# A decoder layer on one core: reordering the seven-product units of the second feed-forward product, and moving the input squares

## The chip, the cores and the metric

The kernel runs on one core of one Trainium2 chip. Its time is device microseconds of an execution, the median of several runs. Before the change three runs gave 1564.54 us in the median (1560.53 to 1565.82).

## What is computed

One layer of a decoder, for 256 tokens of width 2048, in float32. The reference, cut to what matters:

```
u = rms_norm(x, pre_mix_gain)
z = u @ w_in                       # 2048 -> q, k, v, conv value and gate, two mixer gates (7 x 2048)
o = rms_norm(diff_attention(rope(q), rope(k), v, lam)) * (1 - 0.2)   # 8 heads, causal
c = c_val * sigmoid(c_gate)        # then a causal depthwise filter of 31 taps
c = silu(layer_norm(conv31(c))) @ w_conv_out + b
m = sigmoid(ga) * o + sigmoid(gc) * c
h = x + rms_norm(m @ w_out)
u = rms_norm(h, pre_ff_gain)
f = square(relu(u @ w_ff1)) @ w_ff2      # 2048 -> 8192 -> 2048
out = h + rms_norm(f)
```

## The kernel before, in words

**Products.** Each float32 operand is split into a high part of the type fp32r and a low part, the rest; a product is made of three matmuls (high x high, low x high, high x low). A weight comes from memory in chunks of 128 x 2048 numbers (1 MB). A chunk goes through four steps: a DMA on SP's queue into one of three buffers `raw` (L137); a cast on ScalarE into one of three buffers `wh` (L143); a subtraction on VectorE into one of three buffers `wl` (L149), below called the lo-split; and the matmuls. `fill()` (L195) traces the next chunks until three are alive, `done()` (L214) gives one back and calls `fill()`. A raw buffer can be loaded again when its cast and its lo-split have read it. `ws_pair` (L266) takes two chunks, 2 x 32 matmuls, for two column blocks of an output; `as_block` and `as_part` (L281) take four chunks for 512 columns of both token tiles.

**Order.** All is traced in program order, and the library's planner then sets each engine's order by priority (program order, shifted by `high_priority(offset)`) and by its own estimate of when operands are ready. On the chip each engine works off its order. `pin` (`keep_in_program_order`) ties an instruction behind the one that was traced just before it on the same engine.

**Lead-in.** The first two chunks and the input are loaded in pieces and multiplied at once (L395 to L410). Then `done()`, the load of `vec`, `done()`, which trace the third, fourth and fifth chunk; then the squares of the input (L425), their sums `xss` (L427 to L429), a matmul with `ones` (L431), two small ones (L434) and the reciprocal roots `rb` and `rt` (L435). A loop over 16 column pairs follows (L478 to L487): `ws_pair`, the copy-out `z` (`ws_sum`, L278 and L279, two buffers), a multiplication by `rb` (L482), a sigmoid (L483), and a filter of 31 taps on VectorE with low priority (L471).

**Second feed-forward product.** It is done in four stages q. In each, eight `ws_pair` make the squared activations `g` of 2048 hidden columns, in `sc` (L844); then two blocks m of 1024 output columns are made with `fast_pair` (L770; in the last stage the second block is made with `as_block`). A `fast_pair` goes over four groups of 512 hidden rows in the order 0, 2, 1, 3. Groups 2 and 3 are plain: two chunks each of 24 matmuls (L815 to L817). Groups 0 and 1 are units of seven products A1 to A7 in place of eight, after Strassen and Winograd: the two raw chunks of a unit are w11, w21 (first) and w12, w22 (second), four sums are made of them on VectorE, and of the activations too (`put_fast`, L760). Seven halves of a weight buffer are cast (L159) and lo-split (L160), in four parts that each take one `wh` and `wl` buffer (`fast_part`, L168):

| part | first half | second half | also made |
|---|---|---|---|
| 0 | w11 for A1 | t1 = w11 + w12 for A5 | w12 += w22 |
| 1 | w12 for A7 | t2 = w12 + w11 for A6 | |
| 2 | w21 for A2 | t4 = t2 + w21 for A4 | |
| 3 | w22 for A3 | | both raw buffers given back |

Each product is 6 matmuls of 512 columns (L793 to L795). A1, A5, A7 and A6 have accumulators of their own (`own`), which ScalarE and VectorE copy out after the second unit (L798 to L803); A2, A4 and A3 add to those of the plain chunks, which are copied out at the end (L819 to L822). All eight banks of PSUM are used by one `fast_pair`, and the next takes the same ones over. From the second stage on, the result is added to `acc` by two DMAs on POOL's queue (L825).

Of the kernel before, what the change touches and what calls it, by code (L numbers as in the profile page):

```python
# [11 lines left out]
F32 = mybir.dt.float32  # L12
# [47 lines left out]
def tile_layer(ctx, tc, x, x_t, pre, vecs, lams, rope_t, subln, b_conv, post_mix, post_ff,  # L60
# [107 lines left out]
    def fast_part(part, i):  # L168
        state["next"] += 1
        state["live"] += 1  # L170
        w11, w21 = quads(raw_tile(i))
        w12, w22 = quads(raw_tile(i + 1))
        wt = (whp.tile([P, CHUNK], F32R, name="wh"), wlp.tile([P, CHUNK], F32R, name="wl"))
        queue.append(wt)

        def new_sum(name, a, b):
            sums[name] = sump.tile([P, 2, 512], F32, name="sum")
            return add(sums[name], a, b)

        if part == 0:  # L180
            split_sum(wt, 0, w11)
            split_sum(wt, 1, new_sum("t1", w11, w12))
            add(w12, w12, w22)
        elif part == 1:
            split_sum(wt, 0, w12)
            split_sum(wt, 1, new_sum("t2", w12, w11))
        elif part == 2:
            split_sum(wt, 0, w21)
            split_sum(wt, 1, new_sum("t4", sums["t2"], w21))
        else:  # L190
            split_sum(wt, 0, w22)
            release_raw(i)
            release_raw(i + 1)

# [71 lines left out]
    def ws_pair(acts):  # L266
        ps = new_ps()
        for j in range(2):
            wh, wl = take()
            for k in range(KT):  # L270
                nc.tensor.matmul(ps[:, j], wh[:, k * P:(k + 1) * P], acts.both(k), start=(k == 0), stop=False)  # L271
            for k in range(KT):
                nc.tensor.matmul(ps[:, j, S:], wl[:, k * P:(k + 1) * P], acts.hi(k), start=False, stop=(k == KT - 1))  # L273
            done()
        return ps
# [136 lines left out]
    done()  # L412
    pin(nc.sync.dma_start(vec, vecs))
    done()

    def vcol(ct, r):
        return vec[:, ct, r:r + 1]
# [4 lines left out]
    with tc.high_priority(offset=CHAIN):  # L422
        for j in range(4):
            sq = xsp.tile([P, 4, S], F32, name="xsq", bufs=2) if j else xss
            pin(nc.scalar.activation(sq, xt[:, 4 * j:4 * j + 4], AF.Square))  # L425
            if j:
                pin(nc.vector.tensor_tensor(xss, xss, sq, op=ALU.add))  # L427
        pin(nc.vector.tensor_tensor(xss[:, 0:2], xss[:, 0:2], xss[:, 2:4], op=ALU.add))
        pin(nc.vector.tensor_tensor(xss[:, 0], xss[:, 0], xss[:, 1], op=ALU.add))  # L429
        pb = aux_ps()[:, 0:S]  # L430
        nc.tensor.matmul(pb, ones, xss[:, 0], start=True, stop=True)  # L431
        pc = aux_ps()[:, 0:NT]
        for t in range(NT):
# [14 lines left out]
    pin(nc.sync.dma_start(rope_sb, rope_t))  # L448
    sub8 = lnp.tile([P, VD], F32, name="sub8")
    pin(nc.sync.dma_start(sub8, subln.partition_broadcast(P)))  # L450
    lam_in = lnp.tile([P, 4, HD], F32, name="lam_in")
    pin(nc.sync.dma_start(lam_in, lams.partition_broadcast(P)))
# [25 lines left out]
    for ct in range(KT):  # L478
        ps = ws_pair(ua) if ct else lead_ps
        z = tmpp.tile([P, 2, S], F32, name="z")  # L480
        ws_sum(z, ps)
        nc.vector.tensor_tensor(z, z, rb2, op=ALU.mult)  # L482
        nc.scalar.activation(z[:, 1], z[:, 1], AF.Sigmoid, bias=vcol(ct, V_GG))  # L483
# [250 lines left out]
    sump = ctx.enter_context(tc.tile_pool(name="sump", bufs=2))  # L734
# [35 lines left out]
    def fast_pair(ga, q, m):  # L770
# [11 lines left out]
        for kc in FF_ORDER:  # L782
            if kc < FAST:
                for pair in ((A1, A5), (A7, A6), (A2, A4), (A3,)):
                    wh, wl = take()
                    for half, a in enumerate(pair):
                        ps = own[a] if a in own else shared[a]
                        for i in range(2):
# [4 lines left out]
                            nc.tensor.matmul(ps, g[:, 0, a], wh[:, sl], start=first, stop=False)  # L793
                            nc.tensor.matmul(ps, g[:, 0, a], wl[:, sl], start=False, stop=False)  # L794
                            nc.tensor.matmul(ps, g[:, 1, a], wh[:, sl], start=False, stop=last)  # L795
# [8 lines left out]
            else:  # L804
                for i in range(2):
                    wh, wl = take()
                    for kk in range(4):
                        k = kc * 4 + kk
                        sl = slice(kk * 512, (kk + 1) * 512)
                        for t in (1, 0):  # L810
# [4 lines left out]
                            nc.tensor.matmul(ps, ga.hi(k, a, b), wh[:, sl], start=first, stop=False)  # L815
                            nc.tensor.matmul(ps, ga.hi(k, a, b), wl[:, sl], start=False, stop=False)  # L816
                            nc.tensor.matmul(ps, ga.lo(k, a, b), wh[:, sl], start=False, stop=last)  # L817
# [19 lines left out]
    for q in range(NQ):  # L837
        ga = Mixed()
        for j in range(KT // 2):
# [4 lines left out]
            sc = fin2.tile([P, 8, P], F32, name="sc")  # L844
# [106 lines left out]
```

## Time and profile before

| | |
|---|---|
| runs, median | 1564.54 us |
| the profiled execution | 1565.17 us, span 1563.4 us |
| TensorE (PE) busy | 1530.4 us |
| its weight loads (PEld) | 1299.7 us |
| VectorE (DVE) busy | 1272.5 us |
| ScalarE (ACT) busy | 769.1 us |
| memory traffic | 306.31 MB, mean 196 GB/s |
| second product, four stages | from 932.85, 1110.06, 1288.48 and 1465.97 us on |

Times in rows are microseconds from the start of the span. A row of the timeline has the start, the length, the engine and the line, and in brackets how long the engine had been idle and what ended it. In the chain of waits a piece counts only until the next piece begins, so a matmul of a back-to-back row stands there with its pitch and not with its modelled length.

### The profile page before, as it was taken

The page shows a single profiled execution, that of the slowest core. Times are in us where ns is not written, and L with a number is a line of the kernel's source. Part 1 is how long each engine was busy: PE and PEld are TensorE (multiplying, and loading weights), DVE is VectorE, ACT ScalarE, POOL GpSimd, SP SyncE. Part 2 cuts the span into 40 slices and gives each one's busy share as a digit, 9 for nine tenths or more (in the row PEclk, how much of TensorE's full clock was granted, in tenths as well). Part 3 has the DMA queues.
Part 4 walks back from the last instruction along what each step waited for, and adds up shares of the span by engine and source line. Part 5 has one row for each costly group of instructions (what it writes and reads, how often), then busy time and mean ns, then how long its engine had stood idle before and what let it go on. Part 6 is the DMA issues. An engine that isn't in the chain of part 4 may idle for free.

```text
span 1563.4 us, 19364 instructions
## 1 busy us (share of the span) xinstructions
PE 1530.4 (98%) x7746; PEld 1299.7 (83%) x7746; DVE 1272.5 (81%) x1609; ACT 769.1 (49%) x812; POOL 17.9 (1%) x44
## 2 busy tenths in 40 slices
PE   9899999999999999999999999999999999899997
PEld 8788888888888888888887887788877888688876
DVE  7899999999999996956547888867887779877775
ACT  7344454646554545734446545544445445544452
POOL 0000000000000000000000000000000000000000
PEclk9999999999999999999999999999999999999999
DMA  8455555544444555575555645555366535575572
GB/s 303 179 192 190 189 188 187 186 166 176 175 167 179 204 200 188 191 269 187 188 191 194 230 148 194 217 211 190 137 220 230 222 136 215 191 267 189 218 253 82
DMA packets 47450, 306.31 MB, mean 196 GB/s; under 512 B 5376, under 2 KB 5504, under 8 KB 12672
## 3 DMA queue, kind: packets, MB, share of 16 engines
q1 hardware_dynamic: 43920, 289.61, 51.0%
q0 software_dynamic: 3008, 14.68, 3.7%
q8 instruction: 60, 0.98, 0.2%
q10 hardware_dynamic: 432, 0.79, 0.2%
q14 instruction: 30, 0.25, 0.0%
HBM read 295.62 MB, written 4.19 MB: 192 GB/s over the span
## 4 chain that ended last, share of the span: by engine, by line
PE 86%; DVE 6%; DMA 5%; ACT 2%; issue 1%; SPq 0%; DVEq 0%; ACTq 0%
PE ps L271 29%; PE ps L273 15%; PE ps L287 10%; PE ps L288 10%; PE ps L289 10%; DMA raw<-in_w_f_dram 4%; PE ps L816 2%; PE ps L817 2%; DVE wl L160 2%; PE ps L815 2%; DVE wl L149 2%; ACT wh L143 1%; DVE sum L165 1%; PE ps L793 1%; PE ps L795 1%; PE ps L794 1%
## 5 line engine op out<-in xcount | busy, mean ns | idle before, releaser
L143 ACT CAST wh<-raw 128x2048 fp32r<-128x2048 f32 (+2 forms) x264 | 467.8, 1780 | 550.2 <-PE ps L271 181.3
L149 DVE TENSOR_TENSOR wl<-raw,wh 128x2048 fp32r<-128x2048 f32 (+2 forms) x264 | 560.6, 2129 | 193.2 <-ACT wh L143 187.8
L271 PE MATMUL ps<-act,wh 128*128 128x512 f32 x1984 | 480.9, 393 | 4.9 <-DVE z L279 4.6
L271 PEld LDWEIGHTS ps<-act,wh 128*128 128x128 f32 x1984 | 365.4, 189 | 76.0 <-issue 4.7
L273 PEld LDWEIGHTS ps<-act,wl 128*128 128x128 f32 x1984 | 256.4, 191 | 9.9
L273 PE MATMUL ps<-act,wl 128*128 128x256 f32 x1984 | 264.0, 284 | 0.0
L289 PE MATMUL ps<-wh,act 128*128 128x512 f32 x624 | 244.0, 391 | 0.0
L287 PE MATMUL ps<-wh,act 128*128 128x512 f32 x624 | 243.7, 391 | 0.0
L288 PE MATMUL ps<-wl,act 128*128 128x512 f32 x624 | 243.3, 390 | 0.0
L471 DVE SCALAR_TENSOR_TENSOR y_all<-c,vec,y_all 128x256 f32<-128x256 f32 x480 | 210.1, 483 | 0.0
L289 PEld LDWEIGHTS ps<-wh,act 128*128 128x128 f32 x624 | 117.1, 188 | 24.3
L287 PEld LDWEIGHTS ps<-wh,act 128*128 128x128 f32 x624 | 117.2, 188 | 24.1
L288 PEld LDWEIGHTS ps<-wl,act 128*128 128x128 f32 x624 | 117.2, 188 | 23.7
L815 PE MATMUL ps<-wh,g 128*128 128x512 f32 x224 | 89.0, 397 | 8.4 <-ACT wh L143 8.4
L816 PE MATMUL ps<-wl,g 128*128 128x512 f32 x224 | 90.2, 403 | 4.4 <-DVE wl L149 4.0
L159 ACT CAST wh<-raw 128x1024 fp32r<-128x1024 f32 x56 | 58.8, 1051 | 66.6 <-PE ps L271 26.7
L817 PE MATMUL ps<-wh,g 128*128 128x512 f32 x224 | 88.4, 395 | 0.0
L160 DVE TENSOR_TENSOR wl<-raw,wh 128x1024 fp32r<-128x1024 f32 x56 | 68.3, 1222 | 11.7 <-PE ps L273 10.8
L794 PE MATMUL ps<-wl,gs 128*128 128x512 f32 x196 | 76.4, 390 | 0.0
L795 PE MATMUL ps<-wh,gs 128*128 128x512 f32 x196 | 76.3, 389 | 0.0
L793 PE MATMUL ps<-wh,gs 128*128 128x512 f32 x196 | 72.9, 391 | 2.0 <-ACT wh L159 2.0
L159 ACT CAST wh<-sum 128x1024 fp32r<-128x1024 f32 x42 | 44.0, 1049 | 47.1 <-DVE sum L165 47.1
(215 smaller groups left out, 1295.5 us busy)
## 6 DMA issues: line engine op xcount, KB each, us to landing
raw<-in_w_f_dram SPq DMA_DIRECT2D x124, 1024.0 KB, 4.9
raw<-in_w_q_dram SPq DMA_DIRECT2D x16, 1024.0 KB, 4.9
raw<-in_w_k_dram SPq DMA_DIRECT2D x16, 1024.0 KB, 4.9
raw<-in_w_v_dram SPq DMA_DIRECT2D x16, 1024.0 KB, 4.9
raw<-in_w_ga_dram SPq DMA_DIRECT2D x16, 1024.0 KB, 4.8
raw<-in_w_gc_dram SPq DMA_DIRECT2D x16, 1024.0 KB, 4.8
raw<-in_w_co_dram SPq DMA_DIRECT2D x16, 1024.0 KB, 4.8
raw<-in_w_o_dram SPq DMA_DIRECT2D x16, 1024.0 KB, 4.8
```

Source lines behind the costliest of these rows:

```text
L143: i = nc.scalar.copy(wh[:, a:b], raw[:, a:b])
L149: i = (eng or nc.vector).tensor_sub(wl[:, a:b], raw[:, a:b], wh[:, a:b].bitcast(F32))
L159: nc.scalar.copy(hi, src)
L271: nc.tensor.matmul(ps[:, j], wh[:, k * P:(k + 1) * P], acts.both(k), start=(k == 0), stop=False)
L273: nc.tensor.matmul(ps[:, j, S:], wl[:, k * P:(k + 1) * P], acts.hi(k), start=False, stop=(k == KT - 1))
L287: nc.tensor.matmul(ps, acts.hi(k, a, b), wh[:, sl], start=(k == 0), stop=False)
L288: nc.tensor.matmul(ps, acts.hi(k, a, b), wl[:, sl], start=False, stop=False)
L289: nc.tensor.matmul(ps, acts.lo(k, a, b), wh[:, sl], start=False, stop=(k == KT - 1))
L471: i = nc.vector.scalar_tensor_tensor(y, c[:, j:j + S], vcol(ct, V_DW + j), y, op0=ALU.mult, op1=ALU.add)
L815: nc.tensor.matmul(ps, ga.hi(k, a, b), wh[:, sl], start=first, stop=False)
L816: nc.tensor.matmul(ps, ga.hi(k, a, b), wl[:, sl], start=False, stop=False)
L817: nc.tensor.matmul(ps, ga.lo(k, a, b), wh[:, sl], start=False, stop=last)
```

## The change

- Parts 0 to 3 of a unit hold A1 and A2, A7 and A3, A5 and A6, and A4. Part 0 reads only the first raw chunk; part 1 makes all four sums and its two halves and gives both raw buffers back; parts 2 and 3 only cast and lo-split sums that are there. The matmuls take the products in that order. `sum` has three buffers instead of two, `sc` one instead of two.
- All matmuls of `fast_pair` are pinned.
- The copy-outs of the first of a block's two column halves (L819, L820) are traced after the first of the last two plain chunks.
- Lead-in: one chunk is traced by `fill()`, then `vec`, then the squares (with a higher priority), then the two `done()`, then the first `ws_pair` of the loop, pinned, and only then the matmuls with `ones`, the first of them pinned. The loads of the rope table, `sub8` and `lam_in` are tied behind the gate of the fifth column pair.

```diff
     def fast_part(part, i):
         state["next"] += 1
         state["live"] += 1
-        w11, w21 = quads(raw_tile(i))
-        w12, w22 = quads(raw_tile(i + 1))
+        if part < 2:
+            w11, w21 = quads(raw_tile(i))
+            w12, w22 = quads(raw_tile(i + 1))
...
         if part == 0:
             split_sum(wt, 0, w11)
-            split_sum(wt, 1, new_sum("t1", w11, w12))
-            add(w12, w12, w22)
+            split_sum(wt, 1, w21)
         elif part == 1:
-            split_sum(wt, 0, w12)
-            split_sum(wt, 1, new_sum("t2", w12, w11))
-        elif part == 2:
-            split_sum(wt, 0, w21)
-            split_sum(wt, 1, new_sum("t4", sums["t2"], w21))
-        else:
-            split_sum(wt, 0, w22)
+            new_sum("t1", w11, w12)
+            split_sum(wt, 0, add(w12, w12, w22))
+            split_sum(wt, 1, w22)
+            new_sum("t2", w12, w11)
+            new_sum("t4", sums["t2"], w21)
             release_raw(i)
             release_raw(i + 1)
+        elif part == 2:
+            split_sum(wt, 0, sums["t1"])
+            split_sum(wt, 1, sums["t2"])
+        else:
+            split_sum(wt, 0, sums["t4"])
...
-    def ws_pair(acts):
+    def ws_pair(acts, pinned=False):
...
     vec = const.tile([P, KT, NV], F32, name="vec")
-    done()
+    fill()
     pin(nc.sync.dma_start(vec, vecs))
-    done()
...
-    with tc.high_priority(offset=CHAIN):
+    with tc.high_priority(offset=CONV_LATE):
         for j in range(4):
             sq = xsp.tile([P, 4, S], F32, name="xsq", bufs=2) if j else xss
             pin(nc.scalar.activation(sq, xt[:, 4 * j:4 * j + 4], AF.Square))
...
         pin(nc.vector.tensor_tensor(xss[:, 0], xss[:, 0], xss[:, 1], op=ALU.add))
+    done()
+    done()
+    next_ps = ws_pair(ua, pinned=True)
+    with tc.high_priority(offset=CONV_LATE):
         pb = aux_ps()[:, 0:S]
-        nc.tensor.matmul(pb, ones, xss[:, 0], start=True, stop=True)
+        pin(nc.tensor.matmul(pb, ones, xss[:, 0], start=True, stop=True))
...
-    pin(nc.sync.dma_start(rope_sb, rope_t))
-    pin(nc.sync.dma_start(sub8, subln.partition_broadcast(P)))
-    pin(nc.sync.dma_start(lam_in, lams.partition_broadcast(P)))
...
-        ps = ws_pair(ua) if ct else lead_ps
+        ps = (lead_ps, next_ps)[ct] if ct < 2 else ws_pair(ua)
...
+        if ct == 4:
+            for a, b in ((rope_sb, rope_t), (sub8, subln.partition_broadcast(P)), (lam_in, lams.partition_broadcast(P))):
+                tc.add_manual_dep(nc.sync.dma_start(a, b).ins, gate.ins.name, order_only, reason="not among the first")
...
-    sump = ctx.enter_context(tc.tile_pool(name="sump", bufs=2))
+    sump = ctx.enter_context(tc.tile_pool(name="sump", bufs=3))
...
-                for pair in ((A1, A5), (A7, A6), (A2, A4), (A3,)):
+                for pair in ((A1, A2), (A7, A3), (A5, A6), (A4,)):
...
-                            nc.tensor.matmul(ps, g[:, 0, a], wh[:, sl], start=first, stop=False)
+                            pin(nc.tensor.matmul(ps, g[:, 0, a], wh[:, sl], start=first, stop=False))
...
-        nc.vector.tensor_tensor(dst(1, 0), plain[1, 0], dst(1, 0), op=ALU.subtract)
-        nc.vector.tensor_tensor(dst(0, 0), plain[0, 0], dst(0, 0), op=ALU.subtract)
+                    if kc == plains[-1] and i == 0:
+                        nc.vector.tensor_tensor(dst(1, 0), plain[1, 0], dst(1, 0), op=ALU.subtract)
+                        nc.vector.tensor_tensor(dst(0, 0), plain[0, 0], dst(0, 0), op=ALU.subtract)
...
-            sc = fin2.tile([P, 8, P], F32, name="sc")
+            sc = fin2.tile([P, 8, P], F32, name="sc", bufs=1)
```

The other five matmul lines of `fast_pair` (L794, L795, L815 to L817) get the same `pin`, and the two of `ws_pair` where `pinned` is set.

## Rows read from the trace of the kernel before

**Rows 1.** The page, part 1: busy us (share of the span) x instructions

```profile
PE 1530.4 (98%) x7746; PEld 1299.7 (83%) x7746; DVE 1272.5 (81%) x1609; ACT 769.1 (49%) x812; POOL 17.9 (1%) x44
```

**Rows 2.** Waits of PE: line <- releaser: us in total, times, longest us

```profile
PE ps L815 <- ACT wh L143: 8.4, 6, 2.2
PE ps L271 <- DVE z L279: 4.6, 1, 4.6
PE ps L816 <- DVE wl L149: 4.0, 9, 1.0
PE ps L793 <- ACT wh L159: 2.0, 2, 1.1
```

**Rows 3.** Windows, the four stages: length, busy of each engine, PEclk, DMA share, GB/s

```profile
932.85:1024.65 91.80, 88.20 (x379) 71.24 (x377) 77.22 (x67) 46.09 (x39) 0.00 (x0) 0.98 0.56 206
1110.06:1203.07 93.01, 88.95 (x379) 71.01 (x378) 76.95 (x67) 45.98 (x39) 2.41 (x4) 0.98 0.61 215
1288.48:1380.56 92.08, 87.57 (x379) 70.18 (x377) 76.92 (x67) 46.24 (x39) 2.35 (x4) 1.00 0.63 217
1465.97:1510.59 44.62, 41.96 (x183) 33.72 (x182) 36.62 (x31) 22.02 (x19) 2.48 (x4) 1.00 0.73 271
```

**Rows 4.** Windows, two short stretches; the column before the last two is PEclk

```profile
1009.63:1013.04 3.41, 3.41 (x9) 2.64 (x9) 1.51 (x2) 1.90 (x1) 0.00 (x0) 0.50 0.91 332
60.73:64.14 3.41, 2.98 (x7) 2.42 (x8) 3.41 (x8) 0.51 (x1) 0.00 (x0) 0.50 0.64 252
```

**Rows 5.** Chain that ended last, lead-in: start us, us, what

```profile
33.47 3.65 PE ps L271 x16
...
49.09 0.43 PE aux L431 x2
...
60.42 0.61 DVE z L279
```

**Rows 6.** Timeline of ACT, lead-in

```profile
20.09 1.91 ACT L143 CAST wh<-raw 128x2048 fp32r<-128x2048 f32 x1 [0.71 <-DMA raw<-in_w_cv_dram]
...
24.37 1.91 ACT L143 CAST wh<-raw 128x2048 fp32r<-128x2048 f32 x1 [1.90 <-DMA raw<-in_w_cg_dram]
...
30.39 1.99 ACT L425 ACTIVATE xsq<-xt 128x1024 f32<-128x1024 f32 x2
```

**Rows 7.** Timeline of DVE, lead-in

```profile
31.77 2.55 DVE L427 TENSOR_TENSOR xss<-xss,xsq 128x1024 f32<-128x1024 f32 x2
...
43.18 0.42 DVE L429 TENSOR_TENSOR xss<-xss 128x256 f32<-128x256 f32 x1
```

**Rows 8.** Groups by line, DVE, first stage: xcount | busy, mean ns | idle before

```profile
L149 DVE TENSOR_TENSOR wl<-raw,wh 128x2048 fp32r<-128x2048 f32 x10 | 22.9, 2289 | 6.4 <-ACT wh L143 6.2
L160 DVE TENSOR_TENSOR wl<-raw,wh 128x1024 fp32r<-128x1024 f32 x14 | 17.1, 1221 | 3.0 <-PE ps L273 2.4 <-ACT wh L159 0.5
...
L165 DVE TENSOR_TENSOR sum<-raw 128x1024 f32<-128x1024 f32 x6 | 7.3, 1222 | 3.2 <-DMA raw<-in_w_f_dram 3.2
```

**Rows 9.** Groups by line, ACT, first stage

```profile
L159 ACT CAST wh<-raw 128x1024 fp32r<-128x1024 f32 x13 | 13.6, 1049 | 6.9 <-DMA raw<-in_w_f_dram 3.2 <-DVE raw L165 2.1 <-PE ps L795 1.7
```

**Rows 10.** Timeline of PE, first and second stage

```profile
942.39 0.39 PE L815 MATMUL ps<-wh,g 128*128 128x512 f32 x1
...
943.18 0.39 PE L817 MATMUL ps<-wh,g 128*128 128x512 f32 x1
...
1169.81 0.59 PE L793 MATMUL ps<-wh,gs 128*128 128x512 f32 x1 [0.93 <-ACT wh L159]
```

**Rows 11.** Chain that ended last, second stage

```profile
1147.22 0.60 DVE ev L819
...
1149.56 1.14 DVE wl L160
...
1157.59 8.73 DMA raw<-in_w_f_dram
```

**Rows 12.** The page, part 6: loads of the feed-forward weights, count, size, median to landing

```profile
raw<-in_w_f_dram SPq DMA_DIRECT2D x124, 1024.0 KB, 4.9
```

More of the change, by code (lines that the diff above doesn't have):

```diff
@@ L270, in ws_pair @@
             for k in range(KT):
-                nc.tensor.matmul(ps[:, j], wh[:, k * P:(k + 1) * P], acts.both(k), start=(k == 0), stop=False)
+                a = nc.tensor.matmul(ps[:, j], wh[:, k * P:(k + 1) * P], acts.both(k), start=(k == 0), stop=False)
+                if pinned:
+                    pin(a)
             for k in range(KT):
-                nc.tensor.matmul(ps[:, j, S:], wl[:, k * P:(k + 1) * P], acts.hi(k), start=False, stop=(k == KT - 1))
+                a = nc.tensor.matmul(ps[:, j, S:], wl[:, k * P:(k + 1) * P], acts.hi(k), start=False,
+                                     stop=(k == KT - 1))
+                if pinned:
+                    pin(a)
             done()
@@ L482, in tile_layer @@
         nc.vector.tensor_tensor(z, z, rb2, op=ALU.mult)
-        nc.scalar.activation(z[:, 1], z[:, 1], AF.Sigmoid, bias=vcol(ct, V_GG))
+        gate = nc.scalar.activation(z[:, 1], z[:, 1], AF.Sigmoid, bias=vcol(ct, V_GG))
         c = cpool.tile([P, CW - 1 + S], F32, name="c")
@@ L792, in fast_pair @@
                             last = a in own and kc == fasts[-1] and i == 1
-                            nc.tensor.matmul(ps, g[:, 0, a], wh[:, sl], start=first, stop=False)
-                            nc.tensor.matmul(ps, g[:, 0, a], wl[:, sl], start=False, stop=False)
-                            nc.tensor.matmul(ps, g[:, 1, a], wh[:, sl], start=False, stop=last)
+                            pin(nc.tensor.matmul(ps, g[:, 0, a], wh[:, sl], start=first, stop=False))
+                            pin(nc.tensor.matmul(ps, g[:, 0, a], wl[:, sl], start=False, stop=False))
+                            pin(nc.tensor.matmul(ps, g[:, 1, a], wh[:, sl], start=False, stop=last))
                     done()
@@ L814, in fast_pair @@
                             last = kc == plains[-1] and kk == 3
-                            nc.tensor.matmul(ps, ga.hi(k, a, b), wh[:, sl], start=first, stop=False)
-                            nc.tensor.matmul(ps, ga.hi(k, a, b), wl[:, sl], start=False, stop=False)
-                            nc.tensor.matmul(ps, ga.lo(k, a, b), wh[:, sl], start=False, stop=last)
+                            pin(nc.tensor.matmul(ps, ga.hi(k, a, b), wh[:, sl], start=first, stop=False))
+                            pin(nc.tensor.matmul(ps, ga.hi(k, a, b), wl[:, sl], start=False, stop=False))
+                            pin(nc.tensor.matmul(ps, ga.lo(k, a, b), wh[:, sl], start=False, stop=last))
                     done()
-        nc.vector.tensor_tensor(dst(1, 0), plain[1, 0], dst(1, 0), op=ALU.subtract)
-        nc.vector.tensor_tensor(dst(0, 0), plain[0, 0], dst(0, 0), op=ALU.subtract)
+                    if kc == plains[-1] and i == 0:
+                        nc.vector.tensor_tensor(dst(1, 0), plain[1, 0], dst(1, 0), op=ALU.subtract)
+                        nc.vector.tensor_tensor(dst(0, 0), plain[0, 0], dst(0, 0), op=ALU.subtract)
         nc.vector.tensor_tensor(dst(1, 1), plain[1, 1], dst(1, 1), op=ALU.add)
```

## Prediction

> **What bounds the kernel now.** I read the page's engine shares first. TensorE is busy 1530 us of the span's 1563.4, VectorE 81% [rows 1]. So only time in which TensorE stands still or runs slowly can go. The second view is what TensorE waited for [rows 2]: 4.6 us once, on the copy-out `z` (L279), and 14.4 us (8.4 + 4.0 + 2.0) on split weights, all in the second feed-forward product. Matmul ends are modelled and cover short waits, so I take the loss from lengths instead. Sixteen 512-column matmuls in a row take 3.65 us [rows 5], 0.228 each. One second-product stage is four units of 42 matmuls, eight plain chunks of 24, and 16 matmuls of the next product mixed into it: 376 by the loops (the view counts those across its edges too), or 85.7 us. The windows of the first three stages last 91.80, 93.01 and 92.08 us [rows 3]; the fourth (42 + 24 + 24 + 42 + 49 = 181 matmuls, 41.3 us) 44.62. The losses are 6.1, 7.3, 6.4 and 3.3 us: **23.0 us**.
>
> The lead-in is the other place. The wait of 4.6 us is followed by a stretch at half of TensorE's clock (0.50, the 1.2 GHz level, TensorE having stood idle before it) in which it worked 2.98 us [rows 4], so 1.5 us more are lost: **6.1 us**. The second row there is such a stretch behind a wait of about 2 us [rows 2].
>
> **The lead-in, worked out.** Why that wait: TensorE's fourth pair after the first needs the sum tile whose copy-out was at 60.42, and `z` has two buffers that come free only after the multiplication by `rb`. `rb` needs the squares: first pair of squares at 30.39 on ScalarE [rows 6], last add at 43.18 on VectorE [rows 7], the `ones` matmul at 49.09 [rows 5]. An order pin ties an instruction to the one traced before it on its engine. In the old text that is the cast of the fifth chunk, in the new one the cast of the third, which ends at 20.09 + 1.91 = 22.0 [rows 6]. Four squares at about 1.0 us (1.99 for two) end at 26.0; the three adds at 1.28 us (2.55 for two [rows 7]), and two smaller ones of together about 1.0, can end near 29. TensorE reaches the pinned `ones` matmul at 33.47 [rows 5], so it should not wait, and `rb` comes some 14 us earlier than now. The two `z` buffers then turn over before the third pair ends, and the 6.1 us go.
>
> What the move costs: the four squares stand before the fourth chunk's cast, which began at 24.37 because of its DMA [rows 6] and now begins at 26.0 and ends at 27.9; TensorE wants it at about 27.9. Nothing to 0.2 us. On VectorE the adds push three lo-splits of 2.29 us and the copy-out of the first pair towards 36, while TensorE wants that sum tile at 33.47 plus 0.8 for the small matmuls [rows 5]: 0 to 1.8 us, as the copy-out is put before or after the third split. If the squares' chain took as long from its first instruction as now (30.4 less one square to 43.6, 14.2 us, from 22.0), the pinned matmul would hold TensorE 2.7 us. I take 0.6 us, near the low end, because nothing shown makes VectorE queue that long. **Lead-in: minus 5.5 us (minus 6.1 to minus 1.6).**
>
> Three loads (rope, sub8, lams; 0.64 MB by their shapes) leave SP's queue behind the third chunk and come back behind the fifth column pair's gate; `vec` (0.31 MB) moves up to their place. ScalarE waited 0.71 and 1.90 us for chunks near there [rows 6]; a chunk that lands earlier may return some 0.5 us, but only if these loads shared the engines with it. Later they sit beside weight loads of 4.9 us a megabyte [rows 12], that is 3.1 us, covered by three raw buffers at 5.6 us of TensorE a chunk; their readers come only after the sixteen pairs. Zero; 3.1 us if that cover is gone. One `sc` buffer instead of two: the next pair writes it 11.1 us later, its readers need about 3. Zero. The third `sum` buffer holds t1, t2, t4 at once; otherwise part 2 could not be prepared.
>
> **The units, worked out.** A unit has four adds and seven lo-splits of 1.22 us [rows 8], and seven casts of 1.05 [rows 9]; the change takes away none. Back to back such a VectorE operation counts 1.14 us and a copy-out 0.60 [rows 11]; a plain chunk's split of 2.29 [rows 8] I count as 2.2. What moves is the last reader of its two raw chunks. Now it is the fourth part's split, behind all eleven VectorE operations and behind a weight buffer that TensorE frees late. In the new order it is t4, eight operations in, with its splits one part less and its buffer two parts earlier (2 x 12 x 0.228 = 5.5 us). So the next two loads start 3.4 to 5.5 us earlier. One that started at 1157.59 landed after 8.73 us [rows 11], and a plain chunk and the unit behind it were both late for it. VectorE idled 3.2 us for raw chunks in the first stage's sums alone [rows 8]. The pins also end the mixing: at 1169.81 a unit's first matmul stands in the middle of a plain chunk and holds it up for its own cast [rows 10]; parts then finish together and free no buffer on the way.
>
> What is late next, by a timetable with those durations:
> - *Entry into a plain chunk.* Its buffer is freed when part 1 ends, 2.74 + 1.37 = 4.1 us before it is wanted, and cast plus lo-split take 1.91 + 2.29 = 4.2. The row of before has this already with nothing else late: 942.39 to 943.18 is 0.79 us for two matmuls, 0.33 lost [rows 10]. Fourteen units: 4.6 us stay.
> - *Second raw of a unit.* Its buffer is free with that lo-split, 0.3 us into the plain chunk. Landing 4.9 [rows 12], two adds, a cast, two splits: ready 10.8 us in. It is wanted after two chunks and part 0, 13.9. Slack 3.1 us.
> - *From the first unit pair of a stage into the second.* VectorE has from the first split of the last plain chunks: four copy-outs of the products, a split of 2.2, two lo-splits, two copy-outs, part 1's six, two copy-outs, two lo-splits: 10 x 1.14 + 2.2 + 8 x 0.6 = 18.4 us. TensorE needs the last of them after 10.9 + 5.5 + 1.4 = 17.8, and it starts 0.3 in: 0.9 us late. I take 1.5, since in-order queues lose a little; three stages: 4.5 us. The copy-outs that the change pulls ahead by a chunk keep the accumulator of A2 free; A3's comes free 4.1 us into the unit at the latest.
> - *Accumulators at a stage's start.* A2 and A3 now take theirs in parts 0 and 1; the last pair's copy-out must be done by 4.1 us. Zero to one copy-out of 0.6 [rows 11] a stage; I take 0.1, 0.4 in all.
>
> Left: 4.6 + 4.5 + 0.4 = 9.5 of 23.0. **Units: minus 13.5 us.** Bounds: only the entries stay, minus 18.4; every second raw takes 8.73 us, plus 5.6 (below).
>
> **Sum.** The profiled execution took 1565.17 us (span 1563.4 and 1.8 around it), 0.6 above the median of 1564.54, which I leave uncorrected. 1565.2 - 5.5 - 13.5 = **1546.2**, say 1546.
>
> **Rivals.**
> - *VectorE keeps the stage as long as it is.* For it: in the first window it is busy 77.22 of 91.80 us [rows 3], and its work stays. Then raws come earlier and only wait, and the lead-in alone is won: 1559.7. Against it: it idled 14.6 us there, and a unit with two chunks and four copy-outs needs 11 x 1.14 + 2 x 2.2 + 4 x 0.6 = 19.3 us of it, for TensorE's 90 x 0.228 = 20.5. The Trainium skill ("Perfetto Trace Analysis", Identifying the Most-Contended Engine) judges TensorE by its weight loads and the others by occupancy; by that, VectorE (84%) is ahead of TensorE (71.24 us, 78%) in that window, and 1559.7 would be the time.
> - *Half.* The planner sets sums ahead of splits that TensorE wants, about half an operation (0.6 us) in each of 14 units: 8.4 us less gain, 1554.6.
> - *More.* Only the entries stay, and the lead-in returns whole: 1565.2 - 18.4 - 6.1 = 1540.7.
> - *Slower: the second raw is late.* All of part 1 now hangs on it. If it lands after 8.73 us as in [rows 11], it is 0.7 us late in eleven units and 3.8 later at three crossings: 19.1 us more than the timetable, 28.6 for 23.0. Each crossing then waits over 5 us and draws a half-clock stretch of 3.4 us, which costs 1.7 [rows 4], three times: 1565.2 - 5.5 + 5.6 + 5.1 = 1570. It decides from a landing above 8 us on. Against it: 8.73 was a load beside another and beside accumulating stores; the median is 4.9 [rows 12].
>
> **Numbers.** Forecast (1541 to 1551) 0.55; half 0.17; more 0.08; VectorE-bound 0.12, split 0.05 faster and 0.07 within, as 0.3% (what can be told from no change here) is 4.7 us and its 1559.7 lies on that border; slower 0.08. Faster 0.85, same 0.07, slower 0.08. Range 1536 to 1560: it leaves out the slower case and the upper edge of the VectorE one.
>
> **What would show it.** Right: no TensorE wait on L279 and no half clock near 61 us; `ones` matmul near 34; the first three stage windows near 88.5 us; ScalarE no longer waiting several us for a raw chunk after a unit; matmuls of a unit all in a row. Wrong: TensorE waiting in front of part 1 (A7) for its lo-split, or at 33 us for the squares, or VectorE without idle time and the windows still near 92.

## The result, and the profile after

The kernel after takes **1545.61 us** in the median (1544.19 to 1546.44, 4 runs). The kernel before, on the same chip, took 1564.35 (1560.53 to 1565.82). The ratio is 0.9883 [0.9864, 0.9902]: 18.7 us faster, where 18.5 were forecast. The profiled execution took 1545.22 us, its span is 1543.4. All runs below are given beside runs of the kernel before on their own chip, whose medians lay between 1564.35 and 1566.98.

The page, part 1, of the kernel after (the answer to [rows 1]):

```profile
PE 1525.3 (99%) x7746; PEld 1298.5 (84%) x7746; DVE 1272.0 (82%) x1609; ACT 768.6 (50%) x812; POOL 17.7 (1%) x44
```

VectorE does the same work as before (1272.0 for 1272.5 us); only the time around it is gone. Line numbers have moved: L271 is now L274, L279 L287, L793 to L795 L804 to L806, L815 to L817 L826 to L828, L431 L442. What TensorE waited for, in the kernel after (the answer to [rows 2]; total us, times, longest):

```profile
PE ps L805 <- DVE wl L160: 3.1, 3, 1.0
PE aux L395 <- POOL ident masks.py:199: 1.6, 1, 1.6
PE aux L335 <- DVE h_sb L695: 1.5, 2, 1.3
PE ps L827 <- DVE wl L149: 1.4, 3, 0.5
```

No wait is left on the copy-out `z` (4.6 us before), none on a cast of `fast_pair` (8.4 and 2.0 before). The two rows in the middle stood in the kernel before as well.

The four second-product stages, from the first matmul of a unit to the first matmul of the next product, in the kernel after (columns as in [rows 3]):

```profile
926.98:1011.90 84.92, 83.21 (x362) 67.20 (x361) 75.52 (x65) 44.09 (x38) 0.00 (x0) 1.00 0.52 193
1100.94:1186.07 85.13, 83.41 (x362) 67.12 (x361) 75.45 (x65) 44.27 (x38) 1.77 (x2) 1.00 0.59 205
1275.11:1360.04 84.93, 83.21 (x363) 67.19 (x361) 75.49 (x65) 44.31 (x38) 1.72 (x2) 1.00 0.58 205
1449.08:1490.65 41.57, 41.44 (x182) 33.63 (x181) 36.34 (x31) 21.83 (x19) 2.47 (x4) 1.00 0.69 257
```

The 16 matmuls of the next product are no longer mixed into a stage, so these windows hold 360 matmuls instead of 376 (180 in the last); with those 16, 3.65 us, the first three would be 88.6, 88.8 and 88.6 long, near the 88.5 named as a mark. 360 x 0.228 = 82.1 us, 180 are 41.0: the losses are 2.8, 3.0, 2.8 and 0.5, together **9.2 us** where 23.0 were lost and 9.5 forecast. (The pitch of 0.228 is a little too long: a unit's 42 matmuls without a wait take 9.52 us here, from 1165.26 to 1174.78, which is 0.227 each. By that pitch 24.8 us were lost before and 10.9 are lost now; the difference stays the same.) The time went in two places: the first stage begins at 926.98 instead of 932.85 (5.9 us), and the stages lose 13.8 us less. The sum, 19.7, agrees with the spans' 20.0.

How a crossing from one block into the next looks now, second stage. First the loads that were issued in the stretch from 1146 to 1156 (name, queue, count, KB, median us from issue to landing), then the timelines of ScalarE, VectorE and TensorE:

```profile
raw<-in_w_f_dram SPq DMA_DIRECT2D x3, 1024.0 KB, 8.8
```

```profile
1155.59 1.91 ACT L143 CAST wh<-raw 128x2048 fp32r<-128x2048 f32 x1 [3.73 <-DMA raw<-in_w_f_dram]
...
1157.53 2.29 DVE L149 TENSOR_TENSOR wl<-raw,wh 128x2048 fp32r<-128x2048 f32 x1 [3.35 <-ACT wh L143]
...
1153.38 0.39 PE L826 MATMUL ps<-wh,g 128*128 128x512 f32 x1
1154.24 0.50 PE L827 MATMUL ps<-wl,g 128*128 128x512 f32 x1 [0.47 <-DVE wl L149]
...
1159.62 0.39 PE L826 MATMUL ps<-wh,g 128*128 128x512 f32 x1
1159.88 0.50 PE L827 MATMUL ps<-wl,g 128*128 128x512 f32 x1
```

This is the row to keep in mind. ScalarE still waits 3.73 us for a raw chunk that takes some 8.8 us to land, as the 8.73 of [rows 11]. But TensorE is meanwhile in the first plain chunk (from 1153.38 on), and reaches the late one at 1159.62; its lo-split ends at 1157.53 + 2.29 = 1159.82 and the matmul that reads it starts at 1159.88. The late transfer is still there, against the sign that the prediction named (ScalarE no longer waiting several us for a raw chunk). It is covered, with almost nothing to spare.

The lead-in, chain of waits of the kernel after (start, us, what):

```profile
32.81 3.65 PE ps L274 x16
36.47 1.79 PE ps L278 x15
38.26 0.43 PE aux L442 x2
38.69 0.34 PE aux L445 x4
```

The `ones` matmul is at 38.26 (49.09 in [rows 5]). Two short windows of the kernel after, columns as in [rows 4]: the first is the stretch that ran at half clock before, the second a new one.

```profile
60.73:64.14 3.41, 3.41 (x20) 2.92 (x19) 3.32 (x5) 1.24 (x2) 0.00 (x0) 1.00 0.53 221
832.90:836.31 3.41, 3.41 (x12) 2.63 (x13) 2.85 (x6) 2.69 (x8) 0.00 (x0) 0.52 0.00 0
```

### The profile page after: what moved, and what is told of

Same layout as the page of the kernel before. It is cut to its first block, busy times and chain, and to the rows that moved or that the text cites. A ratio compares the mean times of both kernels' runs of the same rounds, so it can differ in the third digit from the quotient of the medians.

```text
span 1543.4 us, 19352 instructions
## 1 busy us (share of the span) xinstructions
PE 1525.3 (99%) x7746; PEld 1298.5 (84%) x7746; DVE 1272.0 (82%) x1609; ACT 768.6 (50%) x812; POOL 17.7 (1%) x44
## 4 chain that ended last, share of the span: by engine, by line
PE 90%; DVE 5%; ACT 2%; DMA 1%; issue 1%; SPq 0%; DVEq 0%; ACTq 0%
PE ps L274 29%; PE ps L278 15%; PE ps L295 10%; PE ps L296 10%; PE ps L297 10%; PE ps L827 3%; PE ps L828 3%; PE ps L826 2%; ACT wh L143 2%; DVE wl L149 2%; PE ps L806 1%; PE ps L805 1%; PE ps L804 1%; DMA raw<-in_w_cv_dram 1%; DVE wl L160 1%
## 5 line engine op out<-in xcount | busy, mean ns | idle before, releaser
L274 PE MATMUL ps<-act,wh 128*128 128x512 f32 x1984 | 479.1, 392 | 0.2 <-ACT wh L143 0.2
L274 PEld LDWEIGHTS ps<-act,wh 128*128 128x128 f32 x1984 | 364.6, 188 | 70.6 <-ACT wh L143 0.5
L827 PE MATMUL ps<-wl,g 128*128 128x512 f32 x224 | 89.0, 397 | 2.2 <-DVE wl L149 1.4
L828 PE MATMUL ps<-wh,g 128*128 128x512 f32 x224 | 87.4, 390 | 0.0
L826 PE MATMUL ps<-wh,g 128*128 128x512 f32 x224 | 87.2, 390 | 0.0
L805 PE MATMUL ps<-wl,gs 128*128 128x512 f32 x196 | 76.7, 391 | 3.1 <-DVE wl L160 3.1
L806 PE MATMUL ps<-wh,gs 128*128 128x512 f32 x196 | 76.3, 389 | 0.0
L804 PE MATMUL ps<-wh,gs 128*128 128x512 f32 x196 | 76.3, 389 | 0.0
```

Of the source, the lines that this page charges most:

```text
L274: a = nc.tensor.matmul(ps[:, j], wh[:, k * P:(k + 1) * P], acts.both(k), start=(k == 0), stop=False)
L826: pin(nc.tensor.matmul(ps, ga.hi(k, a, b), wh[:, sl], start=first, stop=False))
L827: pin(nc.tensor.matmul(ps, ga.hi(k, a, b), wl[:, sl], start=False, stop=False))
L828: pin(nc.tensor.matmul(ps, ga.lo(k, a, b), wh[:, sl], start=False, stop=last))
```

## The experiments

**One part of the change at a time.** The change falls into three parts: the lead-in, the new distribution of the units (with the copy-outs, `sump` and `sc`), and the pins on the six matmul lines of `fast_pair`. The first four runs put one or two of them into the kernel before.

The lead-in alone:

```diff
-    done()
+    fill()
     pin(nc.sync.dma_start(vec, vecs))
-    done()
...
+    next_ps = ws_pair(ua, pinned=True)
```

> The lead-in edits alone, units and pins of the second product as before. My theory (the wait on the copy-out and the half-clock stretch behind it go): 5.5 to 6.9 us less than before, ratio near 0.996, and no wait of TensorE on the copy-out near 57 us. Rival (the lead-in's gain is given back later, at the row-wise stage near 830 us, where the changed kernel has a half-clock stretch that the old one has not): 4 us or less.

Measured: 1556.69 us, ratio 0.995 [0.9931, 0.997], 9.1 us less. That is more than either expectation. In its trace the first stage begins at 927.55, 5.3 earlier than before, and no copy-out wait is left in what TensorE waited for; the longest row is now

```profile
PE ps L823 <- ACT wh L143: 6.3, 5, 1.4
```

The other 4 us fell in the stages, whose code is that of before: the half-clock stretch of the first row of [rows 4] did not come, for one. So the lead-in's term is 5 to 6 us, and the stages of the old order vary by some us from one traced execution to another.

Units and pins, with the old lead-in:

```diff
-            split_sum(wt, 1, new_sum("t1", w11, w12))
-            add(w12, w12, w22)
+            split_sum(wt, 1, w21)
...
-                            nc.tensor.matmul(ps, g[:, 0, a], wh[:, sl], start=first, stop=False)
+                            pin(nc.tensor.matmul(ps, g[:, 0, a], wh[:, sl], start=first, stop=False))
```

> New units, pins and earlier copy-outs of the second product, the old lead-in. My theory: 13.5 to 14.1 us less than before, ratio near 0.991, and with the lead-in alone it adds up to the whole change. Rival (the two parts help each other): clearly less than 13.

Measured: 1552.81 us, 0.9916 [0.9903, 0.993], 13.0 us less, for 13.5 forecast. With the 5.3 us of the lead-in's trace that is 18.3, the whole change; with the 9.1 of its median it would be too much. The copy-out wait is there as before:

```profile
PE ps L274 <- DVE z L282: 4.6, 1, 4.6
PE ps L797 <- DVE wl L160: 3.1, 3, 1.0
```

The pins alone:

```diff
-                            nc.tensor.matmul(ps, ga.hi(k, a, b), wh[:, sl], start=first, stop=False)
+                            pin(nc.tensor.matmul(ps, ga.hi(k, a, b), wh[:, sl], start=first, stop=False))
```

> Only the matmuls of the second product are pinned; units, buffers and the release of the raw chunks as before. My theory (the late raw chunks are the larger cause, the mixed order of the matmuls the smaller): 3 to 5 us less than before, and ScalarE still waits several us for a raw chunk behind each unit. Rival (the mixed order was the cause, since it frees weight buffers late and so raw chunks late): 10 to 14 us less, and those waits are gone.

Measured: 1563.0 us, 0.9981 [0.997, 0.9993], 2.8 us less. The crossing of the second stage, timelines of ScalarE and TensorE:

```profile
1164.09 1.91 ACT L143 CAST wh<-raw 128x2048 fp32r<-128x2048 f32 x1 [6.38 <-DMA raw<-in_w_f_dram]
...
1166.05 0.50 PE L815 MATMUL ps<-wh,g 128*128 128x512 f32 x1 [0.45 <-ACT wh L143]
1168.38 0.79 PE L816 MATMUL ps<-wl,g 128*128 128x512 f32 x1 [1.82 <-DVE wl L149]
```

The order is the fixed one, but the raw buffer was freed late: the chunk was issued at 1155.44, and TensorE, which had its first plain chunk to do, still waits 2.27 us, and a half-clock stretch follows. In that stage and the third the pins won almost nothing; what they won lies in the first (a table by stages stands further below).

The new units without the pins:

```diff
-                            pin(nc.tensor.matmul(ps, g[:, 0, a], wh[:, sl], start=first, stop=False))
+                            nc.tensor.matmul(ps, g[:, 0, a], wh[:, sl], start=first, stop=False)
```

> New units and earlier copy-outs, without the pins, the old lead-in. My theory: 8 to 11 us less than before. Rival (the mixed order was the cause): 0 to 3 us less, and a product's matmuls still stand inside plain chunks with waits in front of them.

Measured: 1567.81 us, 1.0007 [0.9997, 1.0016]: nothing. Without the pins the new units, and with them the earlier release, are worth nothing in sum. TensorE's waits and, below, its timeline at the same crossing:

```profile
PE ps L818 <- ACT wh L143: 12.0, 7, 4.3
```

```profile
1160.96 0.39 PE L818 MATMUL ps<-wh,g 128*128 128x512 f32 x1
1165.64 0.80 PE L818 MATMUL ps<-wh,g 128*128 128x512 f32 x1 [4.30 <-ACT wh L143]
1166.23 0.63 PE L819 MATMUL ps<-wl,g 128*128 128x512 f32 x1
1166.66 0.63 PE L820 MATMUL ps<-wh,g 128*128 128x512 f32 x1
```

The planner set the first matmul of the *second* plain chunk (1165.64) behind the first matmul of the first one (1160.96). The load is issued 4.2 us into the unit instead of 5.5, but the 5.5 us of work that would cover the rest stand behind the wait. The next matmuls are 0.43 us apart, near twice the usual pitch: a half-clock stretch.

**The release, with the pins kept: a run that tests something else.** In the kernel after, the splits of `w22` are put back into the last part, so that the second raw chunk is given back there. `t4` takes their place in part 1, and A3 and A4 change places in the order of the products:

```diff
-            split_sum(wt, 1, w22)
...
-            release_raw(i + 1)
...
-            split_sum(wt, 0, sums["t4"])
+            split_sum(wt, 0, sums["w22"])
+            release_raw(i + 1)
```

> The changed kernel, with w22 (A3) cast and split in part 3 and t4 (A4) in part 1, so that the second raw chunk of a unit is held until the last part; pins, lead-in and the first raw chunk's release as changed. My theory (with the pins the raw chunk's release still decides what is late behind a unit): 5 to 9 us slower than the changed kernel, 1551 to 1555, with waits of TensorE for a plain chunk or a unit's part in stages two to four. Rival (with the order pinned the release no longer matters): within 2 us of the changed kernel.

Measured: 1564.22 us, 0.9992 [0.9982, 1.0002], 18.6 more than the kernel after: the direction was expected, the size (5 to 9) far too small. TensorE, crossing of the first stage:

```profile
975.30 0.49 PE L804 MATMUL ps<-wh,gs 128*128 128x512 f32 x1 [0.77 <-ACT wh L159]
978.76 0.79 PE L805 MATMUL ps<-wl,gs 128*128 128x512 f32 x1 [2.97 <-DVE wl L160]
```

The wait at 978.76 is for the lo-split of `t4`, which this edit moved into part 1. VectorE's timeline before it:

```profile
974.09 2.35 DVE L160 TENSOR_TENSOR wl<-sum,wh 128x1024 fp32r<-128x1024 f32 x2
976.36 1.22 DVE L160 TENSOR_TENSOR wl<-raw,wh 128x1024 fp32r<-128x1024 f32 x1
977.49 1.22 DVE L160 TENSOR_TENSOR wl<-sum,wh 128x1024 fp32r<-128x1024 f32 x1
```

VectorE's timeline has no gap from 962.43 on; the planner set three lo-splits that are wanted later (974.09 to 977.5) ahead of the one that TensorE stands for, which ends at 978.71. No cast of ScalarE waits for a load at this crossing or at the other two, and here, in the first stage, the two loads at the crossing land after 4.79 and 4.74 us. Each of the three crossings pays this wait of 3.0 us and a half-clock stretch of up to 6.8 us. So the run shows what a sum costs that is wanted too early in VectorE's queue. It does not show what the release is worth, since no raw chunk came late at a crossing.

**Why the load lands late.** The kernel with pins alone, without the two DMAs that add a stage's result to `acc`, so that its output lacks what the later stages would add:

```diff
-        if q:
+        if q == 9:
             for t in range(NT):
                 nc.gpsimd.dma_start(acc[:, t, m * 1024:(m + 1) * 1024]
```

> The old kernel with pins only, as e3, and without the DMAs that add the results of stages two to four to those of the first (that part of the result is left out). My theory (each of them slows the raw load behind the first unit of the second block to a landing of 8.6 us, so that one cover does not do): 6 to 10 us faster than e3, second and third stage losing about 2.6 us as the first stage does in e3. Rival (the second and third stage are longer for another reason, such as the copy-outs into another buffer): within 2 us of e3.

Measured: 1553.13 us, 0.9916 [0.9901, 0.993], 9.9 less than with them. Loads issued from 1150 to 1166, first in the kernel before, with those DMAs, then in this one:

```profile
raw<-in_w_f_dram SPq DMA_DIRECT2D x3, 1024.0 KB, 8.7
y_sb<-ev POOLq DMA_DIRECT2D x2, 512.0 KB, 8.3
```

```profile
raw<-in_w_f_dram SPq DMA_DIRECT2D x4, 1024.0 KB, 5.1
```

Its second and third stage, which accumulate in the kernel before, come down to nearly the bare matmuls (82.1) here:

```profile
1108.03:1191.38 83.35, 83.10 (x363) 67.19 (x361) 75.61 (x65) 44.76 (x38) 0.00 (x0) 1.00 0.59 215
1280.42:1364.14 83.72, 83.11 (x363) 67.19 (x361) 75.70 (x65) 44.74 (x38) 0.00 (x0) 1.00 0.58 212
```

The same edit in three more kernels. The new units without pins:

> The units' new distribution without the pins (the kernel of the run that gave 1567.81), and without the two DMAs that add each later stage's result to acc, so that part of the result is left out. Theory (the order of the planner only costs because the raw chunk behind the crossing unit lands late, and it lands late because of the accumulating DMAs): the load behind the crossing unit lands after about 5 us, the waits of 4.3 us on its cast and the half-clock stretches behind them go, 1551 to 1556. Rival (the planner's mixing of plain and unit matmuls costs by itself): 1562 or more, with the waits still there.

Measured: 1556.31 us, 0.9934 [0.9918, 0.9951], 11.5 less. That is just above the range expected (1551 to 1556). The planner's order at the crossings is the same, but it costs less now; its longest wait there fell from 4.3 to 0.9 us:

```profile
PE ps L818 <- ACT wh L143: 5.5, 7, 0.9
```

The kernel after:

> The kernel after, without the accumulating DMAs (part of the result left out). Theory of the prediction's timetable (what is left at a crossing is VectorE's queue of 18.4 us against TensorE's 17.8, and no transfer): the waits of about 1 us in front of L805 and 0.5 us at L827 stay, 1544 to 1546. Rival (also in the kernel after the late chunk causes the crossing's loss, only covered but for a rest): these waits go, three or four crossings times 1.2 to 1.7 us, 1539 to 1542.

Measured: 1546.39 us, 0.987 [0.9851, 0.9889]: no difference. The waits of 3.1 and 1.4 us on lo-splits are the same to the tenth, though the three loads from 1146 to 1156 now land after

```profile
raw<-in_w_f_dram SPq DMA_DIRECT2D x3, 1024.0 KB, 6.3
```

instead of 8.8. So what is left at a crossing is not the late transfer; the wait's releaser is a lo-split of VectorE, as the timetable had it, and VectorE's timeline in the kernel after has no gap from 1132.19 to 1151.31. And the kernel before:

> The kernel before, without the accumulating DMAs (part of the result left out): what the units lose when no load shares its time with them. Theory (the loads that these DMAs slow down are only a part of the stages' loss; late releases and the mixed order cost as well, as in the first stage, where nothing is accumulated and 6.1 us are lost): stages two and three become as long as the first, 91.8 for 93.0 and 92.1, 1561 to 1565. Rival (the late loads are nearly all of the loss, and pins and release only cover it): about as the kernels with one part of the change and no accumulation, 1553 to 1557.

Measured: 1558.01 us, 0.9943 [0.9929, 0.9957], 8.9 less than the 1566.98 of its chip: between the two expectations and nearer the rival's. TensorE still waits 7.1 us (4 times) for casts of plain chunks there.

All of these together, as ratios to the kernel before, and what the accumulating DMAs cost by their difference (0.001 is 1.6 us):

| | with the accumulating DMAs | without | they cost, us |
|---|---|---|---|
| before | 1 | 0.9943 | 8.9 |
| pins alone | 0.9981 | 0.9916 | 10.2 |
| new units alone | 1.0007 | 0.9934 | 11.4 |
| both, old lead-in | 0.9916 | not run | |
| the whole change | 0.9883 | 0.9870 | 2.0, the intervals overlap |

The traces of the same runs by stage: lengths of the four stages in us, less 0.227 for each matmul of the next product that stands in one. Each is one execution, and in the first stage nothing is accumulated in any kernel.

| | first | second | third | last |
|---|---|---|---|---|
| before | 88.2 | 89.4 | 88.4 | 44.4 |
| pins alone | 84.7 | 88.7 | 88.3 | 46.2 |
| new units alone | 85.8 | 91.4 | 91.2 | 42.7 |
| the whole change | 84.9 | 85.1 | 84.9 | 41.6 |
| before, without the DMAs | 85.6 | 87.2 | 85.4 | 44.6 |
| pins alone, without | 83.7 | 83.4 | 83.7 | 44.5 |
| new units alone, without | 85.9 | 85.9 | 85.8 | 42.7 |
| the whole change, without | 84.8 | 84.9 | 84.9 | 41.6 |

With the matmuls pinned, the new units win nothing in the first stage, 3.6 and 3.4 us in the two that accumulate, and some 4.7 in the last. Without these DMAs they cost 1.1 to 1.5 us in each of the first three and still win 2.9 in the last. There five loads of POOL's queue stand beside the weight loads. First the loads issued from 1452 to 1464 with pins alone and without the accumulating DMAs, then those from 1443 to 1452 in the kernel after, where the weight loads are issued ahead of POOL's:

```profile
raw<-in_w_f_dram SPq DMA_DIRECT2D x3, 1024.0 KB, 9.8
act<-h_keep POOLq DMA_DIRECT2D x4, 512.0 KB, 8.9
```

```profile
raw<-in_w_f_dram SPq DMA_DIRECT2D x2, 1024.0 KB, 5.8
```

**The small terms.** The copy-outs of the first column half back at the end of the block:

```diff
-                    if kc == plains[-1] and i == 0:
-                        nc.vector.tensor_tensor(dst(1, 0), plain[1, 0], dst(1, 0), op=ALU.subtract)
...
+        nc.vector.tensor_tensor(dst(1, 0), plain[1, 0], dst(1, 0), op=ALU.subtract)
```

> The changed kernel, with the copy-outs of the first column half again traced behind the last plain chunk. My theory (A2 needs that accumulator 1.4 us into the next unit, and VectorE is full there): 3 to 8 us slower than the changed kernel, with TensorE waiting on a copy-out at three crossings. Rival (the planner moves them to the same place anyway): the same time.

Measured: 1545.23 us, 0.9863 [0.9848, 0.9878], no change, with the same waits. That edit does nothing.

The three loads of the lead-in in their old place:

```diff
+    pin(nc.sync.dma_start(rope_sb, rope_t))
...
-        if ct == 4:
-            for a, b in ((rope_sb, rope_t), (sub8, subln.partition_broadcast(P)), (lam_in, lams.partition_broadcast(P))):
```

> The kernel after, with the loads of the rope table, sub8 and lam_in back ahead of the loop, behind the loads that stand there on SP's queue, as before. Theory (the step as forecast: where these 0.64 MB stand costs nothing, the lead-in's gain is the earlier squares): the same as the kernel after within 1.5 us, 1544 to 1547, and no copy-out wait of TensorE near 61 us. Rival (part of the lead-in's gain comes from taking them out of the first weight loads' way): 3.1 us at 4.9 us a megabyte go back, 1548 to 1549.

Measured: 1546.39 us, 0.9872 [0.9853, 0.9892]; no difference can be told, and no copy-out wait comes back. Its profiled execution, the slowest of its four (1548.35), does begin the first stage at 929.67, 2.7 us later than the kernel after, all of it lost before 40 us. So the gain of the lead-in is not theirs in the main; that their place costs some us in some executions, near the 3.1 of the rival, is not ruled out.

The entries: the first plain chunk behind each unit is cast and lo-split in two halves (its load stays one):

```diff
+            after_unit = slots[state["next"] - 1][0] == 3
             chunk = load(pieces)
+            if after_unit:
+                pieces = 2
             w = CHUNK // pieces
```

> The changed kernel, with the first plain chunk behind each unit cast and lo-split in two halves. My theory (0.33 us are lost at each of 14 entries because cast and split of a whole chunk take longer than TensorE's work of 4.1 us ahead): 3 to 5 us faster than the changed kernel, near 1541.5. Rival (VectorE's queue is full behind a unit, one more operation makes the next part late): no gain, or slower.

Measured: **1538.94 us**, 0.9828 [0.9814, 0.9843], 6.7 less than the kernel after (6.3 less than the 1545.23 above, measured on the same chip), and the best of all. Its stages, first, second and last of the four, its waits, and its matmul behind the longest wait of the second stage:

```profile
926.74:1009.39 82.65, 81.92 (x363) 67.49 (x361) 75.91 (x69) 44.48 (x42) 0.00 (x0) 1.00 0.54 198
1098.43:1182.22 83.79, 82.21 (x362) 67.42 (x361) 75.79 (x69) 44.45 (x42) 1.77 (x2) 1.00 0.60 207
...
1443.56:1484.39 40.83, 40.83 (x183) 33.79 (x181) 36.64 (x33) 22.13 (x21) 2.48 (x4) 1.00 0.71 259
```

```profile
PE ps L808 <- DVE wl L160: 2.5, 4, 0.7
```

```profile
1156.48 0.50 PE L830 MATMUL ps<-wl,g 128*128 128x512 f32 x1 [0.85 <-DVE wl L149]
```

The four stages sum to 290.53 us against 296.55 in the kernel after: 6.0 us, of which the entries would be 4.6 at the forecast's price; the waits in a unit at a crossing are shorter too (0.7 where they were 1.0). The last stage runs at its matmuls' pitch throughout (180 x 0.227 = 40.8). In the second stage the late chunk shows again: TensorE now comes sooner to the second plain chunk of the crossing and waits 0.85 us for its lo-split.

## Why the prediction was right, and where it was not

**Lead-in, minus 5.5: right in size, the way there only in part.** 5.9 us were won up to the first stage. The squares' chain does not end near 29. The planner put casts and lo-splits between them, as the timelines of ScalarE and VectorE in the kernel after show:

```profile
21.27 1.05 ACT L432 ACTIVATE xss<-xt 128x1024 f32<-128x1024 f32 x1
...
24.77 1.91 ACT L143 CAST wh<-raw 128x2048 fp32r<-128x2048 f32 x1
26.59 1.05 ACT L432 ACTIVATE xsq<-xt 128x1024 f32<-128x1024 f32 x1
...
30.06 2.28 DVE L149 TENSOR_TENSOR wl<-raw,wh 128x2048 fp32r<-128x2048 f32 x1
32.26 0.69 DVE L435 TENSOR_TENSOR xss<-xss 128x512 f32<-128x512 f32 x1
32.86 2.28 DVE L149 TENSOR_TENSOR wl<-raw,wh 128x2048 fp32r<-128x2048 f32 x1
35.06 0.42 DVE L436 TENSOR_TENSOR xss<-xss 128x256 f32<-128x256 f32 x1
```

The step that failed is "can end near 29": it is 35.5, and the upper bound that the text gave beside it (14.2 us from 22.0 on, 36.2) was the better estimate. The 2.7 us that it charged did not come, because the matmul with `ones` did not stand at 33.5: a pin says only what it must follow, and the planner put all but one of the 32 matmuls of the next column block before it. That the late chain cost nothing is luck as far as the working goes: the working did not have this. `rb` was still some 11 us earlier than before, enough for the two `z` buffers. The window near 61 us runs at the full clock. By 831.36, the wait on L335, the kernel is 6.8 us ahead of the kernel before (838.19). About one of these goes back at 833, in a half-clock stretch that the profiled execution of before did not have. (A slip of the prediction: the stretch behind a wait of about 2 us is the first row of [rows 4], and the one of the lead-in the second.)

**Units, minus 13.5: the sum right (13.8 in the trace, 13.0 with the old lead-in), its attribution wrong.** The number is what is lost less what stays, and what stays was priced rightly (below); which part of the change removes the rest does not enter it. The working gave the gain to loads that start 3.4 to 5.5 us earlier, and a sentence at its end to the pins. The runs show that neither part works alone: minus 2.8 for the pins, nothing for the new units, minus 13.0 for both. At the crossing the load starts, counted from the unit's first matmul, 4.1 us in instead of 5.5: 1.4 us, not 3.4 to 5.5 (in the second unit of that stage's first block it is 0.1 instead of 3.2, in that of its second block 2.7 instead of 2.6). What makes it expensive is that it lands after 8.7 us while the stores of the block before accumulate, not after 4.9. Both parts are needed to hide that: the new units, and the first plain chunk's 5.5 us kept ahead of the late one. Against pins alone the load lands 1.2 us sooner behind the unit's first matmul (13.0 for 14.2, as 4.1 + 8.85 and 5.67 + 8.55), and TensorE comes to its chunk 1.4 us later (17.1 for 15.7), because it has stood for VectorE's queue at the crossing. So only about half of the cover there comes from the earlier start of the load. No run changes the release alone.

Without the accumulating DMAs the kernel before gains 8.9 in the median, the kernel after 2.0 at most. By the table of stages only some 5 of the 8.9 lie where these DMAs run; 2.6 lie in the first stage, whose half-clock stretch ([rows 4], first row) did not come. So some 5 to 9 of the 13 us are this late load, hidden. The rest is in the main what the mixing costs without it: pins alone, with no such DMAs, come to 0.9916, the same ratio as pins and new units with them. By the stages the new units are worth something only as a cover for a slow load, of the accumulating DMAs or of the five loads in the last stage, and cost a little where there is none. The Trainium skill ("DMA: Bandwidth & Descriptors", Issuing engines are not separate DMA queues) says that transfers started by different engines run on the same DMA engines and interleave; this trace agrees, with 8.7 us for a load on SP's queue beside POOL's stores and 5.1 without them.

**The slower rival** had the landing time right and its victim wrong. The loads behind a crossing do take 8.8 us, but the one that is late by it is a plain chunk, and by the fixed order TensorE has work until then. The second raw chunk of the next unit is there by 1160.82, when its cast begins; its unit begins at 1165.26. No run here made a unit's raw chunk late, so what that would cost stays open; the run with 1564.22 did not.

**Left over, 9.5: 9.2 (10.9 by the shorter pitch).** Taking the entries' wait away gave 6.0 us in the stages, where 4.6 were charged to them. A crossing has 1.43 us from one start to the next at L805 (1145.24 to 1146.67) and 0.86 at L827 (1153.38 to 1154.24, in the fence above), against 0.23 and an entry's usual 0.46: 1.20 and 0.40, thus 1.6 where 1.5 was taken. By the run without the accumulating DMAs it is no transfer; that it is VectorE's queue is what the releaser in the waits and VectorE's timeline without a gap say. The accumulators cost nothing that the waits show; the copy-outs pulled ahead were no part of that.

**VectorE-bound** is out. In the first stage VectorE is now busy 75.52 of 84.92 us (89%), after 77.22 of 91.80; it was able to work more closely. The Trainium skill ("Perfetto Trace Analysis", Identifying the Most-Contended Engine) judges TensorE by its weight loads and also by MFU, the share of the peak rate that its matmuls reach, which the prediction left out. By weight loads alone (67.20 us, 79%) VectorE would still be ahead there; the measurement decides, and 82.65 us with halves, for 360 x 0.227 = 81.6 of matmuls, show that TensorE's matmuls are the bound. **Half** (1554.6) and **more** (1540.7) lie outside the runs; the second was reached by another edit.

**Still open:** how the 6.7 us of the halves divide among entries, crossings and the half-clock stretch at 833 that its profiled execution did not show, what the release alone is worth, and why the new units alone gain almost nothing even without the accumulating DMAs (0.9934 for 0.9943). In the traces of the last two the stages are 2.5 us shorter in sum, but the first begins 2.1 later (935.99 for 933.91), behind a half-clock stretch near 61 us of 6.83 us where the other has 3.41; one execution of each does not show whether that is always so.

## What to carry to other kernels

A late transfer can be hidden by issuing it sooner and by keeping other work ahead of its reader, and one half alone may buy nothing: before either is judged by itself, look in the trace at what the engine does while the load is under way. When a run is meant to test a release, look in its trace whether anything waits for the load: another wait, made by the same edit, may be what it measures. Price a load at the place where it is issued, beside the stores that run there, and not by its median. And where a chunk goes through two engines before its first use, it can pay to split it in two at that one spot: here 6.7 us, half of what the reordering gave.

## What the runs showed of the hardware

A load of 1 MB lands after 8.7 us (median of three) beside two 512 KB accumulating DMAs of POOL's queue, of which the first landed after 6.1 us and the second after 10.6 in the kernel before, and after 5.1 us in a kernel without them. Beside five plain loads of POOL's queue it took 9.8. A wait of 1.8 to 4.6 us of TensorE was mostly followed by 3.41 or 6.83 us at half its clock (0.50), but not always: one of 2.16 us at 1499.58 in the kernel before was not, and the same three waits near 832 (1.32, 0.20 and 0.44 us) were followed by such a stretch in the kernel after and by none in the kernel with halves. In the kernel before there was none behind them either, but there was one in the kernel before without the accumulating DMAs, whose code is the same up to there.
